# A hybrid decoder layer in one kernel: stored results fetched one a tick, mixed values of the third quarter loaded sooner, four pairs of operands ahead in the MLP, and the norms' matmuls moved

## The chip, the cores and the metric

The kernel runs on one core of a Trainium2 chip, as one launch. The metric is the device time of an execution in microseconds (us); the kernel before takes 2681.94 us, the median of three runs (2681.28 to 2682.01). A core has five engines with a queue of instructions each: PE (matmuls), DVE (vector), ACT (activation), POOL (GpSimd), and SP, which here only issues DMA transfers. Each works its queue in order; semaphores make one wait for another.

## The reference: one decoder layer

The input x has 2048 tokens of width 1024. The layer, with `rms_norm` scaling each token by the inverse root of its mean square:

```python
hn = rms_norm(h, pre_mix_norm[i])
proj = jnp.einsum('btd,dc->btc', hn, w_in[i])
...                       # gated DeltaNet (4 heads) and HGRN2 (4 heads), each with a gated head norm
mix = jnp.concatenate([o_a, o_b], axis=-1)
mix_out = jnp.einsum('btc,cd->btd', mix, w_out[i])
h = h + rms_norm(mix_out, post_mix_norm[i])

u = jnp.einsum('btd,df->btf', rms_norm(h, pre_mlp_norm[i]), w_mlp_up[i])
y = jnp.einsum('btf,fd->btd', jnp.square(jax.nn.relu(u)), w_mlp_down[i])
h = h + rms_norm(y, post_mlp_norm[i])

e = rms_norm(jnp.einsum('bte,ed->btd', p[i], w_ple_proj[i]), ple_norm[i])
gate = jax.nn.sigmoid(jnp.einsum('btd,de->bte', h, w_ple_gate[i]))
h = h + e * gate
```

Everything is float32. The MLP is 4096 wide, and p has 256 columns.

## The kernel before

**Tiles and splits.** Activations are held transposed, as tiles of 128 channels by 512 tokens: eight tiles (`KD`) by four quarters of the tokens (`NQ`, called q0 to q3). A product of full precision is made of three matmuls of rounded numbers: each operand is split in two halves, where ACT rounds (L172, L225) and DVE subtracts (L173, L226), and `product` (L1168) issues high by high, high by low and low by high. So one output tile over eight k blocks is 24 matmuls.

**Ticks.** PE's order is written out by hand. `mm` calls `tick` ahead of every eighth matmul; `later(gen, offsets)` puts a generator in the agenda, and each offset is a tick at which it runs up to its next `yield`. So side work (norms, residuals, loads) is spread between the matmuls by tables of offsets: `OUT_STEPS`, `MLP_STEPS`, `AMID_STEPS`, `A_LAST` and so on. In the MLP and after, SP's order is the order of the code too; in the mixers and the out-projection the orders of DVE, ACT, POOL and SP come from a scheduler, which takes the steps as the code gives them and sorts by its own estimate of when they can run.

**Norms.** `norm_steps` (heads, L272 to L294) and `rstd_steps` (L1191 to L1210) sum squares over the channels by a pair of matmuls with a matrix of ones: `nrm_g` at L279/L280, `nrm_o` and `nrm_y` at L1197/L1198. Their operand `hl_` is the split sum of squares. `nrm_g`'s result goes through DRAM: `sd_g` is stored, loaded back as `m_g`, stored as `rd_g`, broadcast as `rsb_g`, and then `finish` scales the head's output `og_g` (L615) and stores it to `mixd3_3` (L617).

**The out-projection.** `OUT_ORDER` lists the 32 output tiles "qd", q for the quarter, d for the block of columns. Some tiles of q0 are made already among the mixers, and their results `yo0_d` were stored to DRAM (`yod`); the list `finished` names them. The rest is made in a loop over the order. `mix_operands(q)` loads the eight mixed values `mixTq_k` of a quarter and splits them in place (L336, L225, L226), and the weights `raw_outN` (L361) are loaded and split into `w_outN` (L172, L173). At the loop's start q1's operands are loaded; q2's are due at ticks 8, 10, ... 22 and q3's at 15, 17, ... 29. The loop's first entries are the finished tiles: each is loaded back into `yo0_d` (L1402, L1403), all seven at once. When all tiles of a quarter are there, `normed` makes the norm (`nrm_o`, then `r_o`) and the residual: DVE scales `yo` (L1251), POOL issues an accumulating DMA that adds x (L1252), the sum's square enters `acc_h`, and SP stores it as `h1d` (L1255). That store waits for the accumulating DMA, and whatever stands behind it on SP waits too.

**The MLP.** Each half of the tokens (two quarters) goes through Strassen's scheme: seven products of blocks instead of eight. In `up` groups of `hid` are made and stored (L1519). In `down` a loop runs over `ND` = 112 pairs; pair j is a block of down weights `da` (from `dr` or a stored sum `sumd`) and a block of hidden values `db` (from `hid`), and feeds 12 matmuls into four PSUM banks. `down_pair` loads and splits one pair (L1612 to L1630), and the loop calls `down_pair(half, j + LOOK)` ahead of pair j's matmuls. The first `LOOK` pairs are loaded in the last group of `up`, at its steps 2, 4 and 6. The blocks lie in a ring of ten, which is five pairs. Other work is put ahead of chosen pairs by `between`; there `up_operands` makes the second half's operands, for which the normalising factors `rsb_n` of q2 and q3 are broadcast from DRAM. The results' squares are summed on POOL (`acc_y`), and `end` puts the norm `nrm_y` and the residual in the agenda by `MLP_STEPS` (for the half's second quarter) or `AMID_STEPS` (for its first).

Of the kernel before, what the change touches and what calls it, by code (L numbers as in the profile page):

```python
# [48 lines left out]
TOGETHER = ((1, 7), (1, 6))  # L49
OUT_STEPS = (1, 5) + tuple(range(7, 20)) + (29, 31)  # L50
OUT_LAST = (1, 4) + tuple(range(5, 18)) + (19, 23)
MLP_STEPS = (1, 5) + tuple(range(7, 25, 2))
AMID_STEPS = (1, 5) + tuple(range(12, 39, 3))


A_STEPS = ((3, 6, 7, 8, 9, 10, 12, 14) + tuple(range(16, 24)) + (24, 26, 28, 30, 32, 34, 36)
# [9 lines left out]
A_FIRST = (3, 7, 8, 8, 9, 10, 12, 14) + tuple(range(16, 24)) + (24, 26, 29, 32, 34, 36, 37)  # L66

A_LAST = (A_STEPS[:16] + (24, 25, 27, 28, 29, 30, 31) + tuple(range(32, 44))
          + (44, 46, 48, 49, 50, 51, 53, 54))
B_LAST = tuple(range(24, 34)) + (35, 36, 37, 39, 41, 42, 43, 44, 46, 47)  # L70
LAST = 44

# [24 lines left out]
def trunk(ctx, tc, x, xT, pT, vecs, w_in, w_ab, gdn_a_log, gdn_dt_bias, w_out, w_up, w_down,  # L97
# [153 lines left out]
    def spread_load(rd, name, pool=None, tag="rsb", bufs=2):  # L251
        rsb = (pool or st).tile([P, QT], F32, tag=tag, name=f"rsb_{name}", bufs=bufs)
        nc.sync.dma_start(rsb, rd.broadcast_to([P, QT]))
        return rsb
# [77 lines left out]
    def mix_operands(q):  # L332
        xin[q] = []
        for k in range(KD):
            t = next_pool().tile([P, 2, QT], F32R, tag="ring", name=f"mixT{q}_{k}")
            nc.sync.dma_start(plain(t), mixd[q][k])  # L336
            split_in_place(t)
            xin[q].append(t)
            yield
# [817 lines left out]
    def later(gen, offsets):  # L1157
        for o in offsets:
            agenda.setdefault(clock[0] + o, []).append(gen)
# [21 lines left out]
    def ytile(name):  # L1181
        return f2.tile([P, QT], F32, tag="y", name=name, bufs=16)
# [115 lines left out]
    def start_operands(half):  # L1298
        tops[half] = {n: [] for n in ("11", "3", "1", "2", "21", "4", "22")}
# [40 lines left out]
    def up_operands(half, rsb):  # L1340

        qs = (2 * half, 2 * half + 1)
        start_operands(half)
        for k in range(KD // 2):
            n = f"{half}_{k}"
            b11, b21, b12, b22, t3, t2, t4 = (once(lambda i=i: ytile(f"b{i}_{n}")) for i in range(7))
            for b, s, kk in ((b12, 1, k), (b22, 1, k + KD // 2), (b11, 0, k), (b21, 0, k + KD // 2)):
                nc.sync.dma_start(b(), h1d[qs[s]][kk])
                V.scalar_tensor_tensor(b(), b(), col(R_PREMLP + kk), rsb[s], ALU.mult, ALU.mult)
            yield  # L1350
            moving(half, "11", k, b11())
            V.tensor_tensor(t3(), b22(), b12(), ALU.subtract)
            V.tensor_tensor(b12(), b12(), b11(), ALU.subtract)
            yield
            moving(half, "3", k, t3())
            moving(half, "1", k, b12())
            yield
            V.tensor_tensor(t2(), b22(), b12(), ALU.subtract)
            moving(half, "2", k, t2())
            moving(half, "21", k, b21())  # L1360
            yield
            V.tensor_tensor(t4(), b21(), t2(), ALU.subtract)
            moving(half, "4", k, t4())
            moving(half, "22", k, b22())
            yield
# [29 lines left out]
    made, held = {q: [None] * KD for q in range(NQ)}, {}  # L1395
    mix1 = mix_operands(1)
    run(mix1)
    later(mix_operands(2), range(8, 24, 2))
    later(mix_operands(3), range(15, 31, 2))
    for j, (q, d) in enumerate(order):  # L1400
        if j in finished:
            made[q][d] = ytile(f"yo{q}_{d}")  # L1402
            nc.sync.dma_start(made[q][d], yod[q][d])  # L1403
            continue
        for n in range(2, len(tile_of)):
            if ready_at(n) == j:
                ready_out(n)
        for n in range(3, len(tile_of)):
            if stage_at(n) == j:
                stage_out(n)  # L1410
        if j == len(order) - 5:
            u_raw = [wp.tile([P, 2, QT], F32, tag="raw", name=f"u_raw{i}", bufs=2) for i in range(2)]
            a1, a2 = w_up[0], w_up[FF // P // 2]
            for t, i, src in ((u_raw[0], 0, a1[:, : KD // 2]), (u_raw[1], 1, a1[:, KD // 2 :]),
                              (u_raw[0], 1, a2[:, : KD // 2]), (u_raw[1], 0, a2[:, KD // 2 :])):
                nc.sync.dma_start(t[:, i].rearrange("p (k n) -> p k n", n=P), src)
        if j == len(order) - 2:
            two_blocks(("11", u_raw[0][:, 0]), ("12", u_raw[1][:, 1]))
        if j == len(order) - 1:
            (a11, a21), (s1, s4) = ((t[:, 0], t[:, 1]) for t in u_raw)  # L1420
            b22 = two_blocks(("22", s1), None)
            V.tensor_tensor(s1, s1, a21, ALU.add)
            V.tensor_tensor(a21, a11, a21, ALU.subtract)
            V.tensor_tensor(a11, s1, a11, ALU.subtract)
            V.tensor_tensor(s4, s4, a11, ALU.subtract)
            u_block("3", b22, a21)
            later(prep, range(3 * KD // 2))
        if early is None and h1_r[0] is not None:
            early = early_operands()
            later(early, range(0, 12, 2))  # L1430
        if prep is None and h1_r[1] is not None:
            run(early)
            prep = rest_operands(h1_r[1])
            later(prep, range(3 * KD // 2))
        if j in held:
            ps = held.pop(j)
        elif order[j] == TOGETHER[0]:
            held = {j + i: bank(f"mmo_{q}_{d}_{i}", pp) for i in range(len(TOGETHER))}
            sides = [columns(ready[load_of[i]]) for i in held]
            for k in range(KD):  # L1440
                for i, w in zip(held, sides):
                    product(held[i], w[k : k + 1], xin[q][k : k + 1], k == 0, k == KD - 1)
            ps = held.pop(j)
        else:
            ps = bank(f"mmo_{q}_{d}", pp)
            product(ps, columns(ready[load_of[j]]), xin[q])
        y = ytile(f"yo{q}_{d}") if q < 2 else tp.tile([P, QT], F32, tag="stg", name=f"yo{q}_{d}")
        S.activation(y, ps, AF.Copy)
        acc = square_sums[q] = squares(square_sums[q], ps, d, f"o{q}")
        made[q][d] = y  # L1450
        if q >= 2:
            nc.sync.dma_start(yod[q][d], y)
        if all(of != q for of, _ in order[j + 1 :]) and q < 2:
            later(normed(q, made[q], acc, lambda d, q=q: xT[blk(d), tok(q)], R_POSTMIX, h1d[q], "o", "h"),
                  OUT_LAST if q else OUT_STEPS)
        elif all(of != q for of, _ in order[j + 1 :]):
            later(rstd_steps(acc, 1.0 / D, EPS, f"o{q}", row_of(o_r, q), po, wait=True),
                  (8, 13, 17) if q == 2 else (12, 20, 24))
# [147 lines left out]
        DOWN = (("11", "11"), ("12", "21"), ("21", "11"), ("22", "21"), ("11", "12"), ("12", "22"), ("21", "12"),  # L1606
                ("22", "22"))
    ND = len(DOWN) * NG
    LOOK = 3
    ring = {}  # L1610

    def down_pair(half, j):  # L1612
# [173 lines left out]
    for half in range(2):  # L1786
        for g in range(NG):
            if half == 0 and g == 0:
                continue
            between = {}  # L1790
            if g + 1 < NG:
                nxt = {}
                gen = up_weights(half, g + 1, nxt)
                between = {i: [gen] for i in range(7)}
            else:
                pairs = down_pairs(half)
                between = {i: [pairs] for i in (2, 4, 6)}
            if half == 0 and g == 1:
                later(passed(2), list(range(2, 38, 4)) + [40, 46, 50])
            if half == 0 and g == 6:  # L1800
                later(passed(3), list(range(2, 38, 4)) + [40, 46, 50])
            up(half, g, x, between)
            x = nxt
        if half == 0:
            x, nxt = {}, {}
            gen = up_weights(1, 0, x)
            between = {i: [gen] for i in range(1, 8)}
            ops = up_operands(1, [spread_load(h1_r[q], f"n{q}") for q in (2, 3)])
            for i in range(ND - 8, ND - 67, -3):
                between.setdefault(i, []).append(ops)  # L1810
        else:
            gen = first_gates()
            between = {i: [gen] for i in (3, 1)}
            ple = late_embedding((2, 3))
            for j in EMBED_STEPS:
                between.setdefault(ND - j, []).append(ple)
            ops = [gate_operands(0), gate_operands(1)]
            for n, o in enumerate(ops):
                for i in range(56 - 8 * n, 56 - 8 * n - 9, -1):
                    between.setdefault(i, []).append(o)  # L1820
        down(half, between)
        for v in between.values():
            for gen in v:
                run(gen)
        assert not stored
# [104 lines left out]
```

## Time and profile before

| what | value |
|---|---|
| median of three runs | 2681.94 us |
| profiled execution, its own time | 2686.9 us |
| its span | 2685.1 us |
| PE busy | 2646.8 us, 99% of the span, 12745 matmuls |
| DVE, ACT, POOL busy | 73%, 56%, 5% |
| mean granted TensorE clock | 0.997 |
| out-projection loop | from about 1109 us |
| down loops of the two halves | from 1559 us and 2173 us |

In the rows of the profile L1166 is the helper that issues matmuls, so places are told by tile: `mmo<-mixT,w_out` is the out-projection, `d<-db,da` the down product, `u<-t,wu` the up product, `mmg` the gates. A row of the timeline has the start, the duration, engine, line, operation, output and inputs, how many instructions are merged into it, and in brackets how long the engine was idle just before, and for whom. SPq is SP's queue of DMA issues. A row of waits has the total, how many times, and the longest. A row of windows has, for each engine, busy time and count, then the granted clock (1.00 is full), the share of time that the DMA engines were busy, and GB/s.

### The profile page before, as it was taken

How to read it: one execution, taken by the hardware profiler on the slowest of the kernel's cores; microseconds unless marked ns; L12 is line 12 of the kernel's file. 1: busy time of each engine (PE TensorE's matmuls, PEld its weight loads, DVE VectorE, ACT ScalarE, POOL GpSimd, SP SyncE). 2: the span in 40 equal slices, each digit the busy share in tenths (PEclk: the TensorE clock that was granted, in tenths of full speed). 3: DMA queues.
4: the chain of work that ended last, by engine and by line, in shares of the span. 5: the costliest groups of instructions: out<-in, count | busy, mean ns of one | idle time of the engine just before them, and what ended most of it. 6: DMA issues, size and time to landing. Idle time of an engine off the chain costs nothing.

```text
span 2685.1 us, 38292 instructions
## 1 busy us (share of the span) xinstructions
PE 2646.8 (99%) x12745; PEld 2213.1 (82%) x12745; DVE 1966.1 (73%) x4016; ACT 1493.1 (56%) x3025; POOL 136.5 (5%) x147
## 2 busy tenths in 40 slices
PE   8999999999999999999999999999999999999999
PEld 6788888888888888878888888888888888888887
DVE  7777777776677677578988868767877765468775
ACT  6776555465546556556556555555555555555422
POOL 0000000000000000010000000001000001101000
PEclk9999999999999999999999999999999999999999
DMA  8877777667666775683765576666544475677663
GB/s 271 281 242 245 240 257 243 229 229 250 216 207 222 230 214 183 213 231 106 238 208 195 175 235 221 210 205 207 200 169 145 157 235 187 201 243 245 214 214 127
DMA packets 267766, 573.51 MB, mean 214 GB/s; under 512 B 55578, under 2 KB 60152, under 8 KB 250416
## 3 DMA queue, kind: packets, MB, share of 16 engines
q1 hardware_dynamic: 265264, 566.86, 63.7%
q0 software_dynamic: 2304, 4.20, 0.9%
q8 instruction: 101, 1.65, 0.3%
q14 instruction: 97, 0.79, 0.1%
HBM read 410.57 MB, written 160.37 MB: 213 GB/s over the span
## 4 chain that ended last, share of the span: by engine, by line
PE 65%; DMA 4%; issue 3%; ACT 2%; DVE 1%; POOL 1%; SPq 0%; POOLq 0%; ACTq 0%; DVEq 0%
PE u L1166 22%; PE d L1166 18%; PE mm L1134 9%; PE mmg L1166 6%; PE mmo L1166 4%; PE mme L199 1%; POOL acc_y L242 1%; DMA dr<-in_w_down_dram 1%; DMA ud_g<-u_g 1%; DMA da<-sumd 0%; PE at_h L884 0%; DMA gf_g<-gd 0%; DMA raw_out<-in_w_out_dram 0%; PE mmo L1017 0%; DMA sys_g<-ud_g 0%
## 5 line engine op out<-in xcount | busy, mean ns | idle before, releaser
L1134 PE MATMUL mm<-xt,w 128*128 128x512 f32 x3072 | 785.3, 401 | 5.6 <-DVE acc_vg L564 3.1
L1134 PEld LDWEIGHTS mm<-xt,w 128*128 128x128 f32 x3072 | 554.0, 189 | 107.0 <-issue 4.6
L1166 PE MATMUL d<-db,da 128*128 128x512 f32 x2688 | 614.7, 389 | 2.5 <-ACT db L225 1.8
L1166 PEld LDWEIGHTS d<-db,da 128*128 128x128 f32 x2688 | 504.3, 188 | 109.2 <-ACT db L225 3.0
L1166 PE MATMUL u<-t,wu 128*128 128x512 f32 x2604 | 591.5, 389 | 0.0
L1166 PEld LDWEIGHTS u<-t,wu 128*128 128x128 f32 x2604 | 488.7, 188 | 101.8 <-DVE wu L173 0.3
L226 DVE TENSOR_TENSOR db<-db 128x512 fp32r<-128x512 f32 x224 | 160.7, 717 | 44.5 <-ACT db L225 44.2
L1553 DVE TENSOR_TENSOR u<-u,u 128x512 f32<-128x512 f32 x224 | 150.1, 681 | 53.2 <-PE u L1166 51.7
L1166 PE MATMUL mmg<-h2T,wg 128*128 128x512 f32 (+1 forms) x792 | 174.8, 383 | 0.0
L1166 PEld LDWEIGHTS mmg<-h2T,wg 128*128 128x128 f32 x792 | 145.5, 188 | 29.3 <-issue 0.3
L225 ACT ACTIVATE db<-db 128x512 fp32r<-128x512 f32 x224 | 140.8, 629 | 50.2 <-DMA db<-hid 46.7
L1596 ACT ACTIVATE u<-u 128x512 f32<-128x512 f32 x128 | 80.8, 631 | 156.4 <-DVE u L1553 155.7
L173 DVE TENSOR_TENSOR da<-da 128x512 fp32r<-128x512 f32 x128 | 94.8, 740 | 86.1 <-ACT da L172 84.0
L172 ACT ACTIVATE da<-da 128x512 fp32r<-128x512 f32 x128 | 80.6, 629 | 116.5 <-DMA da<-sumd 92.6
L1166 PE MATMUL mmo<-mixT,w_out 128*128 128x512 f32 x600 | 139.6, 393 | 4.5 <-DVE mixT L226 4.1
L1166 PEld LDWEIGHTS mmo<-mixT,w_out 128*128 128x128 f32 x600 | 113.4, 189 | 29.4 <-DVE mixT L226 5.0
L173 DVE TENSOR_TENSOR da<-dr,da 128x512 fp32r<-128x512 f32 x96 | 68.9, 718 | 46.0 <-ACT da L172 44.8
L172 ACT ACTIVATE wu<-a 128x512 fp32r<-128x512 f32 x124 | 75.1, 623 | 45.7 <-DMA a<-in_w_up_dram 44.2
L173 DVE TENSOR_TENSOR wu<-a,wu 128x512 fp32r<-128x512 f32 x124 | 85.6, 692 | 11.1 <-ACT wu L172 11.0
L1597 ACT ACTIVATE u<-u 128x512 f32<-128x512 f32 x128 | 80.4, 628 | 3.1
L172 ACT ACTIVATE da<-dr 128x512 fp32r<-128x512 f32 x96 | 60.5, 630 | 37.2 <-DMA dr<-in_w_down_dram 30.0
L242 POOL TENSOR_TENSOR acc_y<-acc_y,sq_y 128x512 f32<-128x512 f32 x28 | 38.4, 1372 | 764.3 <-ACT sq_y L241 764.3
(394 smaller groups left out, 3841.0 us busy)
## 6 DMA issues: line engine op xcount, KB each, us to landing
w<-cache_in SPq DMA_DIRECT2D x96, 1024.0 KB
db<-hid SPq DMA_DIRECT2D x224, 256.0 KB
cache_in<-w SPq DMA_DIRECT2D x32, 1024.0 KB
hid<-u SPq DMA_DIRECT2D x128, 256.0 KB
da<-sumd SPq DMA_DIRECT2D x128, 256.0 KB
a<-in_w_up_dram SPq DMA_DIRECT2D x124, 256.0 KB
hid<-ht SPq DMA_DIRECT2D x96, 256.0 KB
dr<-in_w_down_dram SPq DMA_DIRECT2D x96, 256.0 KB
```

The source lines that it names most:

```text
L172: S.activation(t[:, 0], raw, AF.Copy)
L173: eng.tensor_tensor(t[:, 1], raw, t[:, 0], ALU.subtract)
L199: PE.matmul(ps, a, b, start=i == 0, stop=i == n - 1)
L225: S.activation(t[:, 0], plain(t), AF.Copy)
L226: V.tensor_tensor(t[:, 1], plain(t), t[:, 0], ALU.subtract)
L242: eng.tensor_tensor(acc, acc, sq, ALU.add)
L1134: PE.matmul(ps, *terms[i], start=i == 0, stop=i == nt - 1)
L1166: PE.matmul(ps, a, b, start=start, stop=stop)
L1553: V.tensor_tensor(c[new], c[old], ps, ALU.add)
L1596: S.activation(c[k], c[k], AF.Relu)
L1597: S.activation(c[k], c[k], AF.Square)
```

## The change

It touches five things. The last head's norm matmuls (`A_LAST`) come one step of the table later. In the out-projection the finished tiles are loaded back by a generator, the first at once and then one a tick, instead of all at once, and q2's operands are due at ticks 3 to 10 instead of every second tick from 8 to 22. In the MLP four pairs are ahead instead of three (`LOOK`), and the fourth is loaded in the last step of the last `up` group. The two broadcasts of `rsb_n` are issued at a step of the operands' generator of its own, in the down loop at j = 4, instead of ahead of the loop. And the norm matmuls `nrm_y` come two ticks later, with the residual's steps of `MLP_STEPS` two ticks later too; those of `AMID_STEPS` stay.

```diff
-MLP_STEPS = (1, 5) + tuple(range(7, 25, 2))
-AMID_STEPS = (1, 5) + tuple(range(12, 39, 3))
+MLP_STEPS = (1, 7) + tuple(range(9, 27, 2))
+AMID_STEPS = (1, 7) + tuple(range(12, 39, 3))
...
 A_LAST = (A_STEPS[:16] + (24, 25, 27, 28, 29, 30, 31) + tuple(range(32, 44))
-          + (44, 46, 48, 49, 50, 51, 53, 54))
+          + (44, 47, 49, 50, 51, 52, 54, 55))
...
         start_operands(half)
+        rsb = rsb()
+        yield
         for k in range(KD // 2):
...
-    later(mix_operands(2), range(8, 24, 2))
+    later(mix_operands(2), range(3, 11))
+
+    def load_back():
+        for j in finished:
+            yield
+            q, d = order[j]
+            made[q][d] = ytile(f"yo{q}_{d}")
+            nc.sync.dma_start(made[q][d], yod[q][d])
+
+    back = load_back()
+    next(back)
+    later(back, range(2, 2 + len(finished)))
     later(mix_operands(3), range(15, 31, 2))
     for j, (q, d) in enumerate(order):
         if j in finished:
-            made[q][d] = ytile(f"yo{q}_{d}")
-            nc.sync.dma_start(made[q][d], yod[q][d])
             continue
...
-    LOOK = 3
+    LOOK = 4
...
-                between = {i: [pairs] for i in (2, 4, 6)}
+                between = {2: [pairs], 4: [pairs], 6: [pairs, pairs]}
...
-            ops = up_operands(1, [spread_load(h1_r[q], f"n{q}") for q in (2, 3)])
-            for i in range(ND - 8, ND - 67, -3):
+            ops = up_operands(1, lambda: [spread_load(h1_r[q], f"n{q}") for q in (2, 3)])
+            for i in (ND - 4, *range(ND - 8, ND - 67, -3)):
                 between.setdefault(i, []).append(ops)
```

On SP, in the out-projection, from the store of the last head's output `mixd3_3` to the load of `raw_out13`, before:

```order
L617 DMA mixd3_3_124<-og_g3_3_12029 128x512
L336 DMA mixT2_6_12426<-mixd2_6_119 128x512
L336 DMA mixT3_6_12539<-mixd3_6_127 128x512
L336 DMA mixT3_7_12562<-mixd3_7_128 128x512
L361 DMA raw_out12_12327<-in_w_out_dram 128x1024
L336 DMA mixT3_3_12453<-mixd3_3_124 128x512
L336 DMA mixT2_7_12469<-mixd2_7_120 128x512
L1255 DMA h1d0_0_129<-yo0_0_12089 128x512
L1255 DMA h1d0_1_130<-yo0_1_12091 128x512
L1255 DMA h1d0_2_131<-yo0_2_12093 128x512
L361 DMA raw_out13_12391<-in_w_out_dram 128x1024
```

The same place after (`raw_out11` and `mixT3_0` to `mixT3_2` stood ahead of `mixd3_3` before):

```order
L336 DMA mixT2_7_12270<-mixd2_7_120 128x512
L361 DMA raw_out11_12302<-in_w_out_dram 128x1024
L336 DMA mixT3_0_12346<-mixd3_0_121 128x512
L336 DMA mixT3_1_12377<-mixd3_1_122 128x512
L336 DMA mixT3_2_12418<-mixd3_2_123 128x512
L1255 DMA h1d0_0_129<-yo0_0_12114 128x512
L336 DMA mixT3_3_12457<-mixd3_3_124 128x512
L361 DMA raw_out12_12343<-in_w_out_dram 128x1024
L1255 DMA h1d0_1_130<-yo0_1_12135 128x512
L336 DMA mixT3_6_12539<-mixd3_6_127 128x512
L1255 DMA h1d0_2_131<-yo0_2_12151 128x512
L361 DMA raw_out13_12403<-in_w_out_dram 128x1024
```

`mixT2_7` stood directly ahead of the store `h1d0_0` and now stands five places ahead of it, while `raw_out12`, which stood three ahead, moved behind that store.

On SP, at the end of the first half's `up`, before (`hid21`, `hid22` are stores of hidden values, `dr` and `db` the loads of pairs 2 to 4):

```order
L1621 DMA dr_0_2_16217<-in_w_down_dram 128x512
L1627 DMA db_0_2_16219<-hid11_0_2_13823 128x512
L1519 DMA hid21_0_15_16225<-u21_0_15_16195 128x512
L1519 DMA hid22_0_15_16243<-u22_0_15_16171 128x512
L253 DMA rsb_n2_16252<-row2_14440 128x512
L253 DMA rsb_n3_16254<-row3_15374 128x512
L1621 DMA dr_0_3_16261<-in_w_down_dram 128x512
L1627 DMA db_0_3_16263<-hid11_0_3_14011 128x512
L1621 DMA dr_0_4_16282<-in_w_down_dram 128x512
L1627 DMA db_0_4_16284<-hid11_0_4_14205 128x512
```

And after:

```order
L1632 DMA dr_0_2_16217<-in_w_down_dram 128x512
L1638 DMA db_0_2_16219<-hid11_0_2_13823 128x512
L1632 DMA dr_0_3_16226<-in_w_down_dram 128x512
L1638 DMA db_0_3_16228<-hid11_0_3_14011 128x512
L1530 DMA hid21_0_15_16234<-u21_0_15_16195 128x512
L1530 DMA hid22_0_15_16252<-u22_0_15_16171 128x512
L1632 DMA dr_0_4_16266<-in_w_down_dram 128x512
L1638 DMA db_0_4_16268<-hid11_0_4_14205 128x512
L1632 DMA dr_0_5_16287<-in_w_down_dram 128x512
L1638 DMA db_0_5_16289<-hid11_0_5_14377 128x512
```

Pair 3 moved ahead of the two stores, and the two broadcasts left this place.

On PE, in the second half's down loop, around the first norm `nrm_y2` (`d1_5_0` to `d1_5_3` are the four output banks, the number behind `db_1_` is the pair), before:

```order
L1166 MATMUL d1_5_0_23696<-db_1_83_23702,da_1_83_23700 128x512 x3
L1166 MATMUL d1_5_1_23697<-db_1_83_23702,da_1_83_23700 128x512
L1197 MATMUL nrm_y2_23775<-hl_y2_23716,ones_94 128x512
L1198 MATMUL nrm_y2_23775<-hl_y2_23716,ones_94 128x512
L1166 MATMUL d1_5_1_23697<-db_1_83_23702,da_1_83_23700 128x512 x2
L1166 MATMUL d1_5_2_23698<-db_1_83_23702,da_1_83_23700 128x512 x3
```

And after:

```order
L1166 MATMUL d1_5_0_23704<-db_1_84_23710,da_1_84_23708 128x512 x3
L1166 MATMUL d1_5_1_23705<-db_1_84_23710,da_1_84_23708 128x512 x3
L1166 MATMUL d1_5_2_23706<-db_1_84_23710,da_1_84_23708 128x512 x2
L1197 MATMUL nrm_y2_23807<-hl_y2_23724,ones_94 128x512
L1198 MATMUL nrm_y2_23807<-hl_y2_23724,ones_94 128x512
L1166 MATMUL d1_5_2_23706<-db_1_84_23710,da_1_84_23708 128x512
L1166 MATMUL d1_5_3_23707<-db_1_84_23710,da_1_84_23708 128x512 x3
```

The pair of norm matmuls moved from pair 83 to pair 84, 16 matmuls later; on PE nothing else moves but the other three `nrm_y` pairs, likewise, and `nrm_g` of the last head, by ten matmuls.

## The prediction

> **What bounds the kernel now.** I read the page's busy list first, then the page's chain of waits, then the list of waits of PE, and last the stretches that this list points to.
>
> ```profile
> span 2685.1 us, 38292 instructions
> PE 2646.8 (99%) x12745; PEld 2213.1 (82%) x12745; DVE 1966.1 (73%) x4016; ACT 1493.1 (56%) x3025; POOL 136.5 (5%) x147
> PE 65%; DMA 4%; issue 3%; ACT 2%; DVE 1%; POOL 1%; SPq 0%; POOLq 0%; ACTq 0%; DVEq 0%
> ```
>
> PE is busy for 99% of the span, so time can only come from PE's idle microseconds, from matmuls at a reduced clock, or go into new idle time of PE. The change alters no count of instructions; it alters who comes when. So the list of PE's waits is the whole budget. These are the rows that the change can reach:
>
> ```profile
> PE mmo L1166 <- DVE mixT L226: 4.1, 2, 3.2
> PE d L1166 <- ACT db L225: 1.8, 3, 1.2
> PE nrm_g L280 <- DVE hl_g L173: 1.5, 2, 1.2
> PE nrm_y L1198 <- DVE hl_y L173: 1.3, 4, 0.6
> PE nrm_y L1197 <- ACT hl_y L172: 1.2, 1, 1.2
> PE d L1166 <- DVE db L226: 0.7, 3, 0.2
> PE mmo L1166 <- DVE w_out L173: 0.4, 1, 0.4
> ```
>
> Columns: total us, times, longest. All of it together is 11.0 us, 0.4% of the span. PE's other rows belong to the start and the mixers, whose code stays. The largest row lies in the out-projection, at the tile "20", the first of the third quarter (PE in order of time, idle time in brackets):
>
> ```profile
> 1108.83 0.50 PE L280 MATMUL nrm_g<-hl_g,ones 128*128 128x512 f32 x1 [1.19 <-DVE hl_g L173]
> ...
> 1152.37 9.63 PE L1166 MATMUL mmo<-mixT,w_out 128*128 128x512 f32 x41 [0.40 <-DVE w_out L173]
> 1162.93 0.97 PE L1166 MATMUL mmo<-mixT,w_out 128*128 128x512 f32 x3 [0.94 <-DVE mixT L226]
> 1167.08 4.15 PE L1166 MATMUL mmo<-mixT,w_out 128*128 128x512 f32 x10 [3.18 <-DVE mixT L226]
> 1171.03 0.42 PE L1197 MATMUL nrm_o<-hl_o,ones 128*128 128x512 f32 x1
> 1171.47 0.50 PE L1198 MATMUL nrm_o<-hl_o,ones 128*128 128x512 f32 x1
> 1171.81 2.49 PE L1166 MATMUL mmo<-mixT,w_out 128*128 128x512 f32 x10
> ```
>
> Undisturbed, 41 matmuls take 9.63 us, 0.23 each. After the 3.18 us wait ten take 4.15, 0.41 each: the stall costs more than its wait. The granted clock (the column before the last two) says so too:
>
> ```profile
> 1160.00:1165.00 5.00, 2.96 (x12) 1.80 (x10) 4.62 (x7) 3.21 (x6) 0.00 (x0) 1.00 0.38 149
> 1165.00:1170.00 5.00, 2.92 (x8) 2.37 (x9) 5.00 (x9) 1.58 (x3) 0.00 (x0) 0.77 0.73 235
> 1170.00:1175.00 5.00, 4.98 (x19) 3.62 (x19) 2.08 (x4) 4.54 (x7) 0.00 (x0) 0.89 0.92 340
> ```
>
> So the price of the low clock is 4.15 − 10 × 0.23 = 1.8 us. The wait's cause is on SP, ACT and DVE (DVE's and ACT's queues run in order):
>
> ```profile
> 1137.37 0.86 SPq L336 DMA_DIRECT2D mixT<-mixd  x2
> 1144.30 4.63 SPq L1255 DMA_DIRECT2D h1d<-yo  x3
> 1149.04 0.93 SPq L361 DMA_DIRECT2D raw_out<-in_w_out_dram  x1
> 1158.77 1.06 ACT L172 ACTIVATE w_out<-raw_out 128x1024 fp32r<-128x1024 f32 x1 [5.30 <-DMA raw_out<-in_w_out_dram]
> 1160.38 0.69 DVE L242 TENSOR_TENSOR acc_h<-acc_h,sq_h 128x512 f32<-128x512 f32 x1 [7.46 <-ACT sq_h L241]
> 1164.00 1.22 DVE L173 TENSOR_TENSOR w_out<-raw_out,w_out 128x1024 fp32r<-128x1024 f32 x1
> 1170.73 0.69 DVE L173 TENSOR_TENSOR hl_o<-acc_o,hl_o 128x512 fp32r<-128x512 f32 x1 [0.69 <-ACT hl_o L172]
> ```
>
> The last mixT2 tiles are loaded at about 1138, but their second split steps stand in DVE's queue behind a square sum, which stands behind ACT, which waits 5.30 us for raw_out13. That weight block was issued at 1149.04 and used at 1158.77, 9.7 us later, behind the stores of h1d0, which wait for POOL's accumulating transfers.
>
> **The out-projection.** (1) The last head's nrm_g pair moves ten matmuls later, 10 × 0.23 = 2.3 us, more than the 1.19 it waits: **−1.2**. Its transfers follow it (POOL's queue keeps its order), but sd_g no longer stands on SP behind seven yo loads, so nothing is late next.
>
> (2) mixT2's eight loads go one a tick (1.83 us) instead of every second tick, among the yo loads; their ACT and DVE steps move with them ahead of the blocked square sum. Both waits at "20" go: **−4.1**.
>
> (3) What is late next is raw_out12. On SP it now stands behind h1d0_0 and mixT3_3 instead of ahead of them, and every queue entry behind it with it. Its use is the split w_out12 on DVE:
>
> ```profile
> 1145.32 1.05 ACT L172 ACTIVATE w_out<-raw_out 128x1024 fp32r<-128x1024 f32 x1
> 1151.10 1.22 DVE L173 TENSOR_TENSOR w_out<-raw_out,w_out 128x1024 fp32r<-128x1024 f32 x1
> ```
>
> Without its 0.40 and the 1.19 of part (1), PE comes for it at 1152.37 − 0.40 − 1.19 = 1150.8. Lower bound: with the shorter queue on DVE it is ready, 0.4 us gained. Upper bound: h1d0_0 still at 1144.30, raw_out12 at 1144.7, 9.7 us as raw_out13 took, 1.06 and 1.22 for the split, ready at 1156.7: a wait of 5.9 in place of 0.4, +5.5. I take ready at 1152, the same moment as now, since SP reaches h1d0_0 earlier without the burst of yo loads, and the transfer's lead shrinks at the same time: **+0.8**.
>
> (4) nrm_o1, 13 matmuls into "20", waits for hl_o1, which was ready at 1170.73 + 0.69 = 1171.42. PE would be there at 1162.93 − 0.94 + 13 × 0.23 = 1165.0. A step on DVE there takes 0.65:
>
> ```profile
> 1168.14 1.29 DVE L226 TENSOR_TENSOR mixT<-mixT 128x512 fp32r<-128x512 f32 x2
> ```
>
> Behind w_out13's split stood eight such steps, now seven; and the split itself no longer comes behind the six steps that DVE does between 1160.38 and 1164.00. If raw_out13 lands as now, w_out13's split runs at 1158.77 + 1.06 = 1159.8, and hl_o1 is ready at 1159.8 + 1.2 + 7 × 0.65 + 1.4 (its own two halves) = 1166.9. It could be ready in time (0), or as now less one step, 1170.8 (a wait of 5.8). I take a wait of 1.5, since raw_out13's issue behind h1d0_2 should come a little sooner, in place of some 0.6 now around its two matmuls: **+0.9**.
>
> (5) The low clock. A wait of 1.19 kept 1.00 in the trace, the 0.94 and 3.18 near each other did not. One of 1.5 is near the first, so most of 1.8 comes back: **−1.4** (0 to −1.8).
>
> The Trainium skill (TensorE: Matmul & The Clock Gate, Part 1, "The HAM clock gate") says that PE falls to half rate after about one idle window of 3.4 us and needs as long busy to return. The trace agrees in kind: 3.18 us idle, then 0.41 instead of 0.23 a matmul; by that rule a wait of 1.5 costs no clock at all, and the term would be −1.8.
>
> Sum of the out-projection: −1.2 − 4.1 + 0.8 + 0.9 − 1.4 = **−5.0**, between −7.9 (all waits and the clock) and about 0.
>
> **The MLP.** (6) Four pairs ahead. Here is the start of the first down loop, PE, then SP and ACT:
>
> ```profile
> 1568.80 0.49 PE L1166 MATMUL d<-db,da 128*128 128x512 f32 x1 [1.21 <-ACT db L225]
> 1569.52 1.65 PE L1166 MATMUL d<-db,da 128*128 128x512 f32 x6 [0.23 <-DVE db L226]
> ...
> 1556.06 3.42 SPq L1519 DMA_DIRECT2D hid<-u  x2
> 1559.53 0.91 SPq L253 DMA_DIRECT2D rsb_n<-row  x2
> 1560.49 0.43 SPq L1621 DMA_DIRECT2D dr<-in_w_down_dram  x1
> ...
> 1567.43 0.63 ACT L172 ACTIVATE da<-dr 128x512 fp32r<-128x512 f32 x1 [5.05 <-DMA dr<-in_w_down_dram]
> ```
>
> Pair 3 is loaded behind two stores of hid and two broadcasts rsb_n. It now stands ahead of all four, and could be issued some 4 us sooner than 1560.49, for a wait of 1.44; it goes. The two broadcasts move to loop step 4, beside running matmuls, and their consumers start at step 8. The same two rows of waits hold 1.8 + 0.7 = 2.5 us in three places; I take all: **−2.5** (0 if the loads only queue on the DMA engines instead of on SP). In the steady loop the ring still holds five pairs, so a load waits for the same matmuls as before; what is later, by up to one pair of 12 × 0.23 = 2.8 us, is the other work on SP, ACT and DVE, which now stands behind one more pair. PE takes from it only h2 and u operands far ahead, so I cost it at 0 here.
>
> (7) The four nrm_y pairs move 16 matmuls later, 3.7 us. They wait 2.5 us in all, at most 1.2 + 0.2 in one place:
>
> ```profile
> 2425.92 0.50 PE L1197 MATMUL nrm_y<-hl_y,ones 128*128 128x512 f32 x1 [1.23 <-ACT hl_y L172]
> ```
>
> hl_y itself can come up to 2.8 us later in the two down loops, behind one more pair's splits on ACT; 3.7 − 1.4 − 2.8 = −0.5 there. So I keep 0.5 of it: **−2.0** (0 to −2.5). The normed values come two ticks later; their readers, the next up operands and the gates, start many ticks behind.
>
> Sum of the MLP: **−4.5**, from 0 to −5.0. Total −9.5. The profiled execution took 2686.9, its span 2685.1; that gives 2677.4 for it. The median of the runs, 2681.9, lies 5.0 below the profiled one; against it the sum gives 2672.4, and I say **2673**.
>
> **Rivals.** *The weights take the wait's place:* raw_out12 and raw_out13 are late by part (3)'s upper bound. Then the out-projection is −1.2 − 4.1 + 5.5 − 0.6, a low clock as now: about −0.4, with the MLP −4.9, 2677. With the MLP's transfers only half relieved, 2680. For it speaks the 9.7 us of raw_out13; against it that raw_out12's split finds its data (no idle time on ACT at 1145.32).
>
> *The MLP part does nothing:* the DMA engines and not SP's order held pair 3. Then −5.0 alone, 2677. Against it: SP issued these loads only at 1560.49.
>
> *Slower:* work that stands one pair later in the down loops holds DVE or ACT. Each of 32 residual steps (four quarters by eight) loads a tile that DVE then waits for, with the next pairs' splits behind it. A stall like that at 1568.80 costs 1.44 us; ten of 32 would be needed (14.4 − 9.5 = +4.9) to end above the present time by more than noise, all of them gives 2719; I price it with twelve, 2681.9 − 9.5 + 17 = 2689. Against it: in the present loops, with less lead, only three such places exist.
>
> **How the numbers follow.** Forecast and what is close to it (2667 to 2676.5): 0.66. Weights late or MLP idle (2676.5 to 2683): 0.24, some of it still faster than the bound. Slower: 0.10. A measurement tells 0.2%, 5.4 us, from no change: faster means under 2676.5, slower over 2687.3. So faster 0.70, same 0.21, slower 0.09. The range reaches down to all of both parts, −7.9 − 5.0 = −12.9, 2669, and 1 for what the terms leave open: 2668; and up through the late weights, 2681.
>
> **What would show it.** nrm_g, nrm_y and "d" vanish from PE's waits; "mmo waits for mixT" vanishes; the row from 1165 to 1170 has a clock of 1.00; a row "mmo waits for w_out" of about 1 us or "nrm_o waits for hl_o" of about 1.5 stands there instead. I am wrong if w_out12 or hl_o1 waits over 4 us with the clock low after it, or if the down loops show rows of waits for db or da that were not there.

## The result, and the profile after

The changed kernel takes 2674.72 us (median of ten runs, 2671.73 to 2677.94); the kernel before, on the same chip, 2682.09 (2681.01 to 2684.71). The ratio is 0.9971, with a 95% interval from 0.9963 to 0.9978: 7.4 us less. The profiled execution is the fastest of the ten, 2671.73 us, and the one profiled before took 2686.9, longer than any of its ten; so the two spans differ by 15.2 us, twice what the medians show.

From the page after:

```profile
span 2669.9 us, 38295 instructions
PE 2639.4 (99%) x12745; PEld 2210.5 (83%) x12745; DVE 1963.1 (74%) x4016; ACT 1491.8 (56%) x3025; POOL 136.4 (5%) x147
L1166 PE MATMUL d<-db,da 128*128 128x512 f32 x2688 | 612.8, 389 | 0.0
```

PE is as full as before, and the idle time in front of the down products (the last column) is zero; before it was 2.5 us, by the same row of the page. The list of PE's waits after, between 1000 and 1250 us:

```profile
PE nrm_o L1197 <- ACT hl_o L172: 2.6, 1, 2.6
PE mmo L1166 <- DVE w_out L173: 1.0, 2, 0.7
PE mmo L1166 <- ACT acc_o L234: 0.7, 1, 0.7
PE nrm_o L1198 <- DVE hl_o L173: 0.2, 1, 0.2
```

In the whole list no row of d or nrm_y is left, so all eleven waits of the MLP are gone. In the out-projection the rows of mixT and nrm_g are gone, and four others stand there. Where they lie, from PE's timeline after:

```profile
1130.17 6.19 PE L1166 MATMUL mmo<-mixT,w_out 128*128 128x512 f32 x26 [0.67 <-ACT acc_o L234]
1136.68 11.20 PE L1166 MATMUL mmo<-mixT,w_out 128*128 128x512 f32 x48 [0.32 <-DVE w_out L173]
1148.59 12.53 PE L1166 MATMUL mmo<-mixT,w_out 128*128 128x512 f32 x54 [0.72 <-DVE w_out L173]
1163.69 0.50 PE L1197 MATMUL nrm_o<-hl_o,ones 128*128 128x512 f32 x1 [2.57 <-ACT hl_o L172]
1164.42 0.50 PE L1198 MATMUL nrm_o<-hl_o,ones 128*128 128x512 f32 x1 [0.22 <-DVE hl_o L173]
```

The 0.72 is w_out12, the 2.57 is hl_o1, both in the places where the prediction set them. The clock stayed up in this execution (windows, the third column from the end):

```profile
1160.00:1165.00 5.00, 2.21 (x9) 1.27 (x9) 3.71 (x7) 3.23 (x7) 0.00 (x0) 1.00 1.01 374
1165.00:1170.00 5.00, 5.00 (x24) 4.14 (x23) 1.31 (x2) 4.91 (x6) 0.00 (x0) 1.00 0.44 166
```

To see where the time went, I cut each profile at the starts of two of PE's matmuls, the first of the out-projection's loop (L1166; before at 1105.28 us, not at about 1109) and the first down product, in us:

| profile of | start and mixers | out-projection and first up | from the first down product to the last matmul |
|---|---|---|---|
| before | 1105.3 | 454.0 | 1121.2 |
| after | 1101.2 | 451.4 | 1112.7 |
| difference | −4.1 | −2.6 | −8.5 |

In the first stage PE runs the same matmuls in the same order in both kernels, so its 4.1 us say how much a profile's span varies by itself. In the experiments below the same stage took 1099.3 to 1104.6. The MLP's 8.5 us are much larger than the waits in the list, and the out-projection's 2.6 are smaller than what was expected.

### The profile page after: what moved, and what is told of

Same layout as the page of the kernel before. It is cut to its first block, busy times and chain, and to the rows that moved or that the text cites. A ratio compares the mean times of both kernels' runs of the same rounds, so it can differ in the third digit from the quotient of the medians.

```text
span 2669.9 us, 38295 instructions
## 1 busy us (share of the span) xinstructions
PE 2639.4 (99%) x12745; PEld 2210.5 (83%) x12745; DVE 1963.1 (74%) x4016; ACT 1491.8 (56%) x3025; POOL 136.4 (5%) x147
## 5 line engine op out<-in xcount | busy, mean ns | idle before, releaser
L1166 PE MATMUL d<-db,da 128*128 128x512 f32 x2688 | 612.8, 389 | 0.0
L1166 PE MATMUL u<-t,wu 128*128 128x512 f32 x2604 | 591.8, 389 | 0.1
L1166 PEld LDWEIGHTS d<-db,da 128*128 128x128 f32 x2688 | 504.5, 188 | 104.8
L1166 PEld LDWEIGHTS u<-t,wu 128*128 128x128 f32 x2604 | 488.6, 188 | 102.3 <-ACT wu L172 0.5
L1166 PE MATMUL mmg<-h2T,wg 128*128 128x512 f32 (+1 forms) x792 | 174.7, 383 | 0.0
L1166 PEld LDWEIGHTS mmg<-h2T,wg 128*128 128x128 f32 x792 | 145.5, 188 | 29.1
L1166 PE MATMUL mmo<-mixT,w_out 128*128 128x512 f32 x600 | 137.9, 390 | 1.7 <-DVE w_out L173 1.0
L1166 PEld LDWEIGHTS mmo<-mixT,w_out 128*128 128x128 f32 x600 | 112.4, 188 | 26.2 <-DVE w_out L173 1.9
```

What stands on the lines that cost most here:

```text
L1166: PE.matmul(ps, a, b, start=start, stop=stop)
```

## Experiments

The kernel before is beside each, on the same chip.

### The parts apart

**MLP alone**: the kernel before with these edits.

```diff
-MLP_STEPS = (1, 5) + tuple(range(7, 25, 2))
-AMID_STEPS = (1, 5) + tuple(range(12, 39, 3))
+MLP_STEPS = (1, 7) + tuple(range(9, 27, 2))
+AMID_STEPS = (1, 7) + tuple(range(12, 39, 3))
...
-    LOOK = 3
+    LOOK = 4
...
-                between = {i: [pairs] for i in (2, 4, 6)}
+                between = {2: [pairs], 4: [pairs], 6: [pairs, pairs]}
```

The two broadcasts rsb_n also go into the down loop, as in the change.

> Only the MLP's parts of the change: four pairs ahead, the two broadcasts in the down loop, the norms nrm_y two ticks later; the out-projection and A_LAST as before. Theory 1 (each stop of PE costs its idle time and about 0.28 us more for PE to get going again, and both parts add): 7.6 us less than before, from the down loop's first matmul to its last 937.7 us as in the changed kernel instead of 945.5, and no wait of d or nrm_y over 0.2 us. Rival (the MLP was not worth more than its waits in the list): 4.5 to 5.0 us less. Rival (the parts give nothing on their own, since the gain is a shift of the start and mixers): within 3 us of the time before.

Measured: 2675.03 us, ratio 0.9972 (0.9962 to 0.9983), 7.5 us less. The last stage took 1113.5 us. It is the first theory's figure; the rival's 4.5 to 5.0 lies at the very end of the interval.

**Out-projection alone**: the kernel before with the loads of `mix_operands(2)` at ticks 3 to 10, the generator that fetches one stored result a tick, and `A_LAST`.

```diff
-          + (44, 46, 48, 49, 50, 51, 53, 54))
+          + (44, 47, 49, 50, 51, 52, 54, 55))
...
-    later(mix_operands(2), range(8, 24, 2))
+    later(mix_operands(2), range(3, 11))
...
+    later(back, range(2, 2 + len(finished)))
```

> Only the out-projection's parts and the last head's norm matmuls (A_LAST); the MLP as before. Theory 1: 3.0 us less than before; from the out-projection's first matmul to nrm_h 69.0 us instead of 72.0, PE waiting 2.6 us for hl_o in nrm_o, about 1.0 for w_out and 0.7 for acc_o; the MLP's eleven waits all there. Rival (the prediction's sum): 5 us less. Rival (the out-projection's gain was chance of one profiled run): within 1 us of the time before.

Measured: 2682.34 us, ratio 0.9998 (0.9989 to 1.0007). The prediction's 5 us are outside the interval, the first theory's 3.0 at its very end, and in this profile the stage took 453.7 us, as before, with 72.0 us up to nrm_h where that theory said 69.0; the last rival, no gain, fits. The wait for mixT is gone here too; what stands there is in its list of waits:

```profile
PE nrm_o L1197 <- ACT hl_o L172: 2.8, 1, 2.8
PE mmo L1166 <- DVE w_out L173: 1.1, 2, 0.8
PE mmo L1166 <- ACT acc_o L234: 0.8, 1, 0.8
PE mmo L1166 <- ACT w_out L172: 0.3, 1, 0.3
```

**Norms alone**: the tables, nothing else.

```diff
-MLP_STEPS = (1, 5) + tuple(range(7, 25, 2))
-AMID_STEPS = (1, 5) + tuple(range(12, 39, 3))
+MLP_STEPS = (1, 7) + tuple(range(9, 27, 2))
+AMID_STEPS = (1, 7) + tuple(range(12, 39, 3))
...
-          + (44, 46, 48, 49, 50, 51, 53, 54))
+          + (44, 47, 49, 50, 51, 52, 54, 55))
```

> Only the norms' matmuls later: MLP_STEPS, AMID_STEPS and A_LAST; the loads as before. Theory 1: nrm_y's four places cost 3.9 us from matmul start to matmul start (2.5 in the list of waits), all of it returned, and nrm_g's 1.6 returned but taken up again by a longer wait for w_out12 in the out-projection, since that block's load is unchanged: 3.9 to 4.3 us less. Rival (list of waits): 2.5 less. Rival (the matmuls' new places hold back later work by two ticks): no gain or a loss.

Measured: 2679.69 us, ratio 0.9988 (0.9979 to 0.9996), 3.2 us less; no wait of nrm_y is left. The size does not tell 2.5 from 4, but a loss is excluded. The stages took 1101.9, 451.3 and 1119.5 us. Tile 20 still waits 3.2 us for mixT, and yet the second stage, with its loads as before, is as short as in the changed kernel.

**The changed kernel once more**, in the same batch:

> The changed kernel once more, beside the other three on one chip, for the sum of the parts and for a second profile. Theory 1: 10.6 us less than before in this batch if the stages alone decide (3.0 and 7.6); the ten runs shown gave 7.4. Rival (some of the stages' gain is lost again in the mixers or elsewhere in most executions): again 7 to 8 us less, with a start and mixers that take longer than the 1101 us of the first profile.

Measured: 2674.42 us, ratio 0.9973 (0.9961 to 0.9984), 7.2 us less. The stages took 1104.6, 450.4 and 1112.7 us, so it is the rival's case in part: the second and third stages gain as in the first profile, the first stage takes what it happens to take. Within the out-projection the waits lie otherwise than in the first profile: w_out12 waits 1.71 and 0.53 us, hl_o1 0.85 and 0.22. The two largest rows of its list there:

```profile
PE mmo L1166 <- ACT w_out L172: 1.7, 1, 1.7
PE nrm_o L1197 <- ACT hl_o L172: 0.9, 1, 0.9
```

The gain by the runs (7.4 and 7.2) is that of the MLP alone (7.5).

**Four pairs ahead alone**: `LOOK`, the load at the last step of up, and the broadcasts; the norms as before.

```diff
-    LOOK = 3
+    LOOK = 4
```

> Only four pairs ahead with the two broadcasts moved into the down loop; the norms and the out-projection as before. Theory 1 (a stop costs 0.28 us more than its idle time): the three starts of the down loops that cost 4.1 us from matmul to matmul in the profile of before (and up to 1.7 more where the clock falls after them) go, nrm_y's four places stay: 4 to 6 us less than before. Rival (one pair more ahead only shifts the waits): the norms' matmuls wait longer, since hl_y stands behind one more pair on ACT, 2 to 3 us less in all. Rival (list of waits): 2.5 less.

Measured: 2675.97 us, ratio 0.9976 (0.9967 to 0.9986), 6.4 us less, and the last stage 1113.9 us, 7.3 under before. The stalls of d went, and nearly all of nrm_y's waits with them, which the first theory had left in place. All that is left in its list from 1500 us on:

```profile
PE nrm_y L1198 <- DVE hl_y L173: 0.2, 1, 0.2
```

The rival said that hl_y would come later behind one more pair. It comes sooner relative to PE: at nrm_y2 ACT's half of it is ready 0.5 us ahead of PE, and before it was 1.2 behind. A possible reason can be seen on ACT and DVE in the kernel before, ahead of nrm_y2's wait at 2425.92:

```profile
2408.08 0.63 ACT L172 ACTIVATE da<-dr 128x512 fp32r<-128x512 f32 x1 [5.61 <-DMA dr<-in_w_down_dram]
...
2415.70 0.69 DVE L173 TENSOR_TENSOR da<-da 128x512 fp32r<-128x512 f32 x1
2416.31 0.68 DVE L1659 TENSOR_TENSOR y<-y,d 128x512 f32<-128x512 f32 x1
2417.03 0.63 ACT L241 ACTIVATE sq_y<-y 128x512 f32<-128x512 f32 x1 [0.70 <-DVE y L1659]
```

One late load of dr holds ACT for 5.61 us, the splits of the next pairs come behind it, the last of them closely, and the sums of the finished product, from which hl_y is made, stand behind them. With four pairs ahead the first of these sums follows a split at once:

```profile
2405.22 0.69 DVE L173 TENSOR_TENSOR da<-da 128x512 fp32r<-128x512 f32 x1 [1.48 <-ACT da L172]
2405.83 0.68 DVE L1661 TENSOR_TENSOR y<-y,d 128x512 f32<-128x512 f32 x1
```

DVE waited for ACT in front of it, so there is no backlog. That the late load caused the wait at 2425.92 is argued, though, and not shown. With the out-projection alone, whose MLP is that of before, a load of dr held ACT as long at the same place, and nrm_y2 hardly waited:

```profile
2404.30 0.63 ACT L172 ACTIVATE da<-dr 128x512 fp32r<-128x512 f32 x1 [5.73 <-DMA dr<-in_w_down_dram]
2421.31 0.50 PE L1198 MATMUL nrm_y<-hl_y,ones 128*128 128x512 f32 x1 [0.18 <-DVE hl_y L173]
```

What is shown is that each part of the MLP takes nrm_y's waits away by itself, so the two can't add in full: 6.4 and 3.2 us alone, 7.5 together by the runs.

### What the out-projection's reordering is worth

**The MLP and A_LAST, with the out-projection's loads as before**: the changed kernel without the fetches one a tick and with q2's operands at ticks 8 to 22. Against the changed kernel:

```diff
-    later(mix_operands(2), range(3, 11))
+    later(mix_operands(2), range(8, 24, 2))
...
-    later(back, range(2, 2 + len(finished)))
...
+            made[q][d] = ytile(f"yo{q}_{d}")
+            nc.sync.dma_start(made[q][d], yod[q][d])
```

> The MLP's parts and the last head's norm matmuls (A_LAST), with the loads of the out-projection as before: the changed kernel without the fetches one a tick and without the mixed values sooner. Theory 1 (the out-projection's reordering only trades the 3.2 us wait for mixT against waits for acc_o, w_out and hl_o1 that cost 4.9 to 5.4): the out-projection stage takes 69 to 70 us, the time is within 1.5 us of the changed kernel's. Rival (the reordering is worth the 3 us of the first pair of profiles): 3 us slower than the changed kernel, 2677.5.

Measured: 2674.43 us, ratio 0.9968 (0.9956 to 0.9981), the same as the changed kernel's 2674.42 on another chip. The stage took 453.5 us in its profile against 451.4 and 450.4, but the times show no difference. Nor does the stage prove one: the norms alone have the same out-projection in their source, with the same `A_LAST`, and took 451.3 us there. So two profiles of one and the same code differ by 2.2 us, nearly as much as the reordering seems to be worth.

**Only q2's mixed values sooner:**

```diff
-    later(mix_operands(2), range(8, 24, 2))
+    later(mix_operands(2), range(3, 11))
```

> Only q2's mixed values sooner (ticks 3 to 10); the stored results still fetched all at once, everything else as before. Theory 1 (the split of mixT2_7 stood behind the blocked square sum, whatever fetched yo): the wait of tile 20 for mixT goes, nrm_o waits for hl_o1 instead, with raw_out12 late: the out-projection stage takes 69 to 72 us, the time within 2 us of before. Rival (both moves are needed): the wait for mixT stays at 2 us or more.

Measured: 2684.07 us, ratio 1.0012 (1.0003 to 1.0021), 3.2 us *more*. The wait for mixT is gone, as by the first theory, but a larger one takes its place:

```profile
1149.58 12.56 PE L1166 MATMUL mmo<-mixT,w_out 128*128 128x512 f32 x54 [1.50 <-DVE w_out L173]
1167.00 0.79 PE L1197 MATMUL nrm_o<-hl_o,ones 128*128 128x512 f32 x1 [4.86 <-ACT hl_o L172]
```

1.50 and 4.86 stand in place of 0.40, 0.94 and 3.18, and the clock fell as well. The stage took 456.6 us.

**Only the stored results one a tick**, with q2's operands as before:

```diff
+    back = load_back()
+    next(back)
+    later(back, range(2, 2 + len(finished)))
...
-            made[q][d] = ytile(f"yo{q}_{d}")
-            nc.sync.dma_start(made[q][d], yod[q][d])
```

> Only the stored results fetched one a tick; q2's mixed values at ticks 8 to 22 as before. Theory 1: tile 20 still waits 3 us or more for mixT, since its split keeps its place behind the square sums; the out-projection stage takes 70 to 73 us, the time within 2 us of before. Rival: sd_g and with it the whole chain of the last head, og_g and h1d0 come some 4 us sooner, raw_out13 too, and the wait goes by that alone.

Measured: 2681.57 us, ratio 1.0005 (0.9996 to 1.0014), the same as before; tile 20 still waits:

```profile
PE mmo L1166 <- DVE mixT L226: 3.2, 1, 3.2
```

So the sooner loads alone remove the wait for mixT and are a loss by themselves; together with the fetches one a tick and `A_LAST` that loss is made up for, and no more.

### Moving the new stops away

**nrm_o of the second quarter two ticks later**, on top of the change:

```diff
-OUT_LAST = (1, 4) + tuple(range(5, 18)) + (19, 23)
+OUT_LAST = (1, 6) + tuple(range(7, 20)) + (21, 25)
```

> The changed kernel with one table more: nrm_o of the second quarter and the residual's steps behind it two ticks later (OUT_LAST from 1, 4, 5 to 17, 19, 23 to 1, 6, 7 to 19, 21, 25). Theory 1 (the wait for mixT gave way to one for hl_o1, which is late because ACT and DVE, in order, wait for raw_out13 and mixT3_7): the 3.3 us between the matmuls around nrm_o1 go, the out-projection stage from its first matmul to nrm_h takes 65.5 us and 1.8 to 3.7 us go by the later place of nrm_h itself, and the time is 2 to 3 us under the changed kernel's. Rival (ACT and DVE are the bound there): nrm_o1 waits as long as now, or the next weight takes the wait; no gain.

Measured: 2674.45 us, ratio 0.9968 (0.9958 to 0.9979). The wait in nrm_o is gone, and no time is gained:

```profile
PE mmo L1166 <- ACT w_out L172: 1.4, 1, 1.4
PE nrm_h L1197 <- ACT hl_h L172: 1.2, 1, 1.2
PE mmo L1166 <- DVE w_out L173: 0.8, 2, 0.5
PE nrm_h L1198 <- DVE hl_h L173: 0.7, 1, 0.7
```

The next norm, nrm_h of that quarter, now waits. w_out12 waits 2.0 us, more than the 0.72 of the changed kernel's first profile and less than the 2.24 of its second. The rival holds in that nothing is gained.

**With the last quarter's mixed values at ticks 20 to 27 as well:**

```diff
-    later(mix_operands(3), range(15, 31, 2))
+    later(mix_operands(3), range(20, 28))
```

> The changed kernel with nrm_o of the second quarter two ticks later and the last quarter's mixed values due at ticks 20 to 27, one a tick, instead of 15 to 29 by two; in the orders that moves mixT3_7's load behind the last stores of h1d0, and its split on ACT behind the squares of tile 10. Theory 1: as with the norm alone, and hl_o1 up to 2 us sooner since ACT no longer waits 1.7 us for mixT3_7 ahead of it; 2 to 4 us under the changed kernel. Rival: the tile 30 waits for mixT3_7 instead, 1 to 3 us lost there.

Measured: 2673.57 us, ratio 0.9966 (0.9954 to 0.9979). No tile waits for mixT3; nrm_h1 and w_out12 wait as in the kernel before this one, and the stage took 452.2 us. The expected 2 to 4 us are not there.

**And nrm_h of the second quarter later too:**

```diff
-OUT_LAST = (1, 6) + tuple(range(7, 20)) + (21, 25)
+OUT_LAST = (1, 6) + tuple(range(7, 20)) + (21, 27)
```

> As the changed kernel with nrm_o of the second quarter two ticks later and the last quarter's mixed values at ticks 20 to 27, and the norm nrm_h of the second quarter two ticks later still (OUT_LAST ends 21, 27 instead of 21, 25). Theory 1 (stops by place): the 2.3 us at nrm_h1 (1.2 and 1.0 from matmul to matmul) go; w_out12's 2.2 and the smaller ones stay: out-projection and the first up products together 143.2 us, 1 us under the changed kernel's 144.0 to 144.2, which the times can hardly show. Rival (each stop that is moved away turns up at the next norm or weight): 144 us or more.

Measured: 2672.14 us, ratio 0.9969 (0.9957 to 0.9980). Up to the norm nrm_h of the first quarter the out-projection takes 65.0 us instead of 69.0 in the changed kernel. But the up products behind it wait now (list of waits, 1240 to 1560 us):

```profile
PE u L1166 <- ACT w_u L172: 1.0, 1, 1.0
PE u L1166 <- DVE wu L173: 0.9, 1, 0.9
PE u L1166 <- ACT wu L172: 0.4, 1, 0.4
PE u L1166 <- DVE w_u L173: 0.3, 1, 0.3
```

The whole second stage took 451.4 us, like the changed kernel's 451.4. In all three, ACT, DVE or a load is what PE meets next between 1130 and 1350 us: a stop that is taken away there turns up later. None of the three variants beats the changed kernel by more than the interval.

## Why the prediction was right, and where not

The time, 2673 forecast and 2674.72 measured, came out of two errors that nearly cancel; the direction follows from the mechanism, but that the total is so close is luck.

**The MLP's term was too small.** −4.5 was the sum; the stage lost 8.5 us in the profile, and the MLP alone 7.5 by the runs (interval 4.6 to 10.2). The stage's figure is steady: 1121.1 to 1122.3 us in the four profiles with the MLP as before, 1112.7 to 1113.9 in the eight with four pairs ahead. The mechanism held: pair 3 ahead of the stores, and nrm_y later, took every wait away. The step that failed is the price of a wait. I took the idle time from the list, but a stop costs more than that. It can be read off the first down loop of the kernel before, from PE's timeline there:

```profile
1563.79 3.79 PE L1166 MATMUL d<-db,da 128*128 128x512 f32 x16
1568.80 0.49 PE L1166 MATMUL d<-db,da 128*128 128x512 f32 x1 [1.21 <-ACT db L225]
1569.52 1.65 PE L1166 MATMUL d<-db,da 128*128 128x512 f32 x6 [0.23 <-DVE db L226]
```

A matmul is shown as 0.39 long (the mean of the page's row), while undisturbed ones start 0.23 apart. So the last of the sixteen started at 1563.79 + 3.79 − 0.39 = 1567.19, and the next starts are 1.61 and 0.72 later; one more gap, of 0.34 inside the last row, is longer than 0.23 too. That is 1.38 + 0.49 + 0.11 = 1.98 too much, for listed waits of 1.21 + 0.23 = 1.44, or 0.27 more at each stop. Of this 0.16 come in because a matmul is shown 0.39 long while the next can start after 0.23, and 0.11 because the first one behind a stop is shown 0.49 long. Eleven waits make 11 × 0.27 = 3.0 on top of 5.0, which is 8.0 of the 8.5. The starts at all eleven places in the profile before confirm it: 4.1 us too much around the six waits of d and 3.9 around the five of nrm_y. In the profile after no two matmuls of this stage start more than 0.30 apart. The allowance of 0.5 for a later hl_y was wrong in its sign: with four pairs ahead hl_y came sooner relative to PE.

**The out-projection's term was too large.** −5.0 was the sum; the stage shows −2.6 in one profile and −3.6 in the next, the runs of it alone −0.5 (interval −3.0 to +1.9). By its parts:
- nrm_g, −1.2: gone as said, though its pair moved by 8 matmuls (1.8 us) and not by ten: PE's timeline has 8 of the loop's matmuls ahead of it before and 16 after.
- mixT, −4.1: gone as said, also with the sooner loads alone.
- w_out12, a wait of 1.2 taken: 0.72 in the first profile and 2.24 in the second, with another 0.32 and 0.27 at w_out10 that I had not listed.
- hl_o1, a wait of 1.5 taken, 0 to 5.8 the bounds: 2.57 and 0.22 in the first profile after, 0.85 and 0.22 in the second, 4.86 with the loads sooner alone. Its pair stands 13 matmuls behind tile 20's first wait, which is what the sum uses, and not 13 into the tile. Its chain was as described, with one step left out: on ACT the split of mixT3_7, which the change moved behind the stores of h1d0, stands ahead of the squares, and ACT waits for it:

```profile
1154.24 1.06 ACT L172 ACTIVATE w_out<-raw_out 128x1024 fp32r<-128x1024 f32 x1 [3.14 <-DMA raw_out<-in_w_out_dram]
1157.57 0.64 ACT L225 ACTIVATE mixT<-mixT 128x512 fp32r<-128x512 f32 x1 [1.74 <-DMA mixT<-mixd]
1163.01 0.63 ACT L172 ACTIVATE hl_o<-acc_o 128x512 fp32r<-128x512 f32 x1 [1.43 <-DVE acc_o L242]
```

- The bank of acc_o, 0.67 and in the second profile 0.32, was not foreseen: ACT frees it behind the first quarter's r_o chain, which now comes ahead of it.
- The clock, −1.4: it stayed at 1.00 there in both profiles of the changed kernel, but that is no property of the change. After a wait of 2.8 in the profile of the out-projection alone, whose out-projection has the same source, the granted clock did fall, to 0.68 between 1163 and 1168 us.

The lower end of −7.9 is not quite the sum of its rows: with the 0.4 of w_out12 and the 0.6 of part (4) it is −8.1, which changes nothing here.

The rival "the weights take the wait's place" has the size that the out-projection alone shows by the runs (−0.4 and −0.5), but not its place: w_out12 waits 1.1 us in that profile, and hl_o1, with 2.84 and 0.22, is the larger part. "The MLP part does nothing" is excluded. "Slower", by work that stands one pair later, is excluded as well: no row of d appears in the lists of the kernels with four pairs ahead.

What stays open is whether the out-projection's reordering is worth anything: its stage is 2 to 3 us shorter in both profiles of the changed kernel than with the MLP and A_LAST alone, equal to before with the out-projection alone, and just as short without any reordering in the profile of the norms alone. The times show no difference.

## What to carry to other kernels

A wait in the list of a full engine is a lower bound of its price: take the distance between the instructions' starts, less their undisturbed pace. Taking away an early wait can take later ones with it: here nearly all of nrm_y's went when only the loads came sooner, so measure the parts apart before adding them up. Where several in-order engines are nearly in step with PE, taking one stop away brings the next one to light; here the gain stayed only where all of a stage's stops went, in the down loops.

## What the runs showed of the hardware

The granted clock after a stop is not settled by the stop's length. Two kernels have the same code at tile 20 and the same wait of 3.18 us. With the MLP's change alone the ten matmuls after it take 2.60 us, with four pairs ahead alone 4.63 (PE's timeline of each):

```profile
1162.30 2.60 PE L1166 MATMUL mmo<-mixT,w_out 128*128 128x512 f32 x10 [3.18 <-DVE mixT L226]
```

```profile
1162.96 4.63 PE L1166 MATMUL mmo<-mixT,w_out 128*128 128x512 f32 x10 [3.18 <-DVE mixT L226]
```

Their waits just before differ (the second kernel has one of 0.96 three matmuls earlier), as in the profile before; but with the norms alone the wait of 3.2 stands by itself, as with the MLP alone, and the clock is 0.66 between 1160 and 1165 us.

What differs is where the stop lies. In the traces' record of the granted clock every change, in all thirteen profiles, falls on a grid with steps of 3.41 us, which lies elsewhere in each execution, and each fall lasts one step or two, at half. Here are the falls of the kernel before and of four pairs ahead alone:

```profile
1167.67:1171.09 3.42, 3.42 (x10) 2.57 (x8) 2.73 (x5) 1.39 (x4) 0.00 (x0) 0.50 1.00 330
```

```profile
1161.79:1168.61 6.82, 5.65 (x13) 4.47 (x14) 4.94 (x9) 3.30 (x7) 0.00 (x0) 0.50 0.95 314
```

With four pairs ahead alone PE was idle for 2.45 us of the step that ends at 1161.79. With the MLP's change alone a border at 1160.72 cuts the 3.18 us in two, 1.6 on either side, and the clock stayed. From 100 us to the last matmul the clock fell eleven times, each time behind a step with 1.5 to 3.4 us of idle PE; no other step has more than 1.7, and between 1.5 and 1.7 both happened.

With the out-projection alone the clock fell after only 1.29 and 0.22 us at the first down loop, both within one step (1560.79 to 1564.20), where it had stayed at 1.00 in the profile before after 1.21 and 0.23:

```profile
1562.60 0.50 PE L1166 MATMUL d<-db,da 128*128 128x512 f32 x1 [1.29 <-ACT db L225]
1563.32 8.97 PE L1166 MATMUL d<-db,da 128*128 128x512 f32 x31 [0.22 <-DVE db L226]
...
1562.00:1568.00 6.00, 5.18 (x14) 3.91 (x15) 3.28 (x6) 3.04 (x6) 0.00 (x0) 0.72 1.04 383
```

The Trainium skill (TensorE: Matmul & The Clock Gate, Part 1, "The HAM clock gate") names an idle window of about 3.4 us and calls the window free-running. The grid of 3.41 us, and that the same stop does or does not lower the clock, fit a free-running window; that 1.5 us in two pieces lowers it does not fit a need for 3.4 us of idleness, and the measurement decides. So a stop of some 1.5 us or more carries a chance of another 1.8 to 2.3 us (the ten matmuls' 4.15 and 4.63 less 2.3), by where it falls on the grid, and a profile with none of them, like the one after, is a favourable one.
